# Zero rows added to the mixer's narrow stationary operands, and a sample state update split by sequence

## The chip, the cores and the metric

One core of a Trainium2 chip runs the whole program. The metric is the device time of one execution in microseconds (us). The engines are TensorE (PE; its weight loads have a row of their own, PEld), VectorE (DVE), ScalarE (ACT), GpSimd (POOL) and SyncE (SP, which issues most DMAs).

## The reference, cut to what matters

One layer of a hybrid decoder runs for a prompt of 1024 tokens (with 16 meta tokens before it) and for 8 sample sequences of 8 tokens. Around the part that changes lie two large feed-forward blocks. The mixer between them has two branches over the same projected input. Branch A is a gated delta rule with 8 heads of 128 x 128 state:

```
def gated_delta_recurrent(q, k, v, beta, g, s0):          # the 8 sample sequences
    def step(s, xs):
        q_t, k_t, v_t, b_t, g_t = xs
        s = s * jnp.exp(g_t)[..., None, None]
        u = b_t[..., None] * (v_t - jnp.einsum('nhd,nhde->nhe', k_t, s))
        s = s + k_t[..., :, None] * u[..., None, :]
        return s, jnp.einsum('nhd,nhde->nhe', q_t, s)
```

The prompt does the same in chunks. Branch B is attention in a window of 128 tokens, where every query also sees the 16 meta keys:

```
o = (jnp.einsum('nbkgqs,nskd->nbqkgd', p[..., :N_META], v_meta)
     + jnp.einsum('nbkgqs,nskd->nbqkgd', p[..., N_META:], vb))       # prompt
o = (jnp.einsum('nkgts,nskd->ntkgd', p[..., :N_META], v_meta)
     + jnp.einsum('nkgts,nskd->ntkgd', p[..., N_META:], v_all))      # samples
```

The outputs are the two results and the new states, among them the sample states after 8 steps for each head and sequence.

## The kernel before, in words

Tokens lie in 9 tiles: 8 of 128 prompt tokens and one of 80 (64 sample tokens, 16 meta tokens). A matmul has a stationary operand of rows x columns (rows are the contraction, held on partitions) and a moving operand that streams through it; the profile writes `48*128 48x256` for 48 rows, 128 columns and 256 moving columns. Operands typed float32r take one pass, float32 ones take two passes, so they appear twice for each call. The large projections split each operand into a high and a low part and make three products (lines L128, L130, L132).

The order of TensorE's instructions is written out by hand: `weave` deals the steps of several generators into one sequence, so that attention blocks or the delta chain lie between steps of a projection. A step is one product of a projection or the stretch of a generator up to its next `yield`. The other engines and the DMA queues are ordered by a planner that simulates the program.

Stages that the change touches, with times of the profile:

- **Window attention, about 1010 to 1330 us.** `window` runs 32 blocks (4 head pairs x 8 tiles), each in `swa_block`, among projections (`swa_q`, later `qv_steps`). In the first two of the four pairs every tenth projection step also lets DVE do a step of the triangular solve (`lane_solve`, L1061 and L1063). In a block the probabilities of the meta keys come in three parts of 16 rows (high, low, high); they are transposed (L1233), copied to `pm` (L1235) and multiplied by `vm`, three times 16 meta values (L1162), as the first product of the group at L1256. Both operands have 48 rows. Sample attention (`swa_sample`, twice, in two halves each) multiplies four sequences per half: for each of four column strips a product with 128 cache rows (L1313) and one with 24 rows of meta and own values (L1314), into the same 32 output rows.
- **Delta heads, about 1345 to 1890 us.** For each head, `chain` first treats the sample tile and then eight prompt tiles, woven with projections, with `prep` and `prep8` of the next head and with `emit` of the one before. In `prep8` the sample keys and queries are packed into `kq` and multiplied (L1504, 64 columns stationary); `kd8`, the decayed keys of the 80 tokens, is loaded (L1490). In `chain`, 16 meta rows of `kd8` start the prompt state (L1551); `p8` of 64 rows gives the sample outputs (L1554), which `normed` writes to rows 64 to 127 of `on8`; POOL writes `xe` (L1561), the solved sample values masked into eight sequences; and after tiles 1 and 3 a product with 64 rows of `kd8` and 512 moving columns of `xe` (L1602) gives the update of four sequence states, which DVE adds (L1604). `emit` transposes the outputs (L1619), for the samples with 64 rows.

Of the kernel before, what the change touches and what calls it, by code (L numbers as in the profile page):

```python
# [649 lines left out]
H = 8  # L650
C_IDENT, C_TRI, C_TRI8, C_BLK8, C_TRIQ, C_MNEG, C_MNEG8 = (i * P for i in range(7))
C_SMASK = 7 * P
C_BASE = C_SMASK + 8
C_BASE0 = C_BASE + 272
C_SBIAS = C_BASE0 + 144
C_W = C_SBIAS + 304
# [2 lines left out]
def constants():  # L659

    r = np.arange(P)
    seq = np.where(r < 64, r // 8, np.where(r < 80, 8, -1))
    live = (r < 80)
    same = (seq[:, None] == seq[None, :]) & live[:, None] & live[None, :]
    le = r[:, None] <= r[None, :]
    cst = np.zeros((P, C_W), np.float32)
    cst[:, C_IDENT:C_IDENT + P] = np.eye(P)
    cst[:, C_TRI:C_TRI + P] = le
    cst[:, C_TRI8:C_TRI8 + P] = le & same
    cst[:, C_BLK8:C_BLK8 + P] = same  # L670
    cst[:64, C_TRIQ + 64:C_TRIQ + P] = (le & same)[:64, :64]
    cst[:, C_MNEG:C_MNEG + P] = np.where(le, 0.0, NEG)
    cst[:, C_MNEG8:C_MNEG8 + P] = np.where(le & same, 0.0, NEG)
    cst[:64, C_SMASK:C_SMASK + 8] = seq[:64, None] == np.arange(8)[None, :]
    i, k = r[:, None], r[None, :]
    own = np.where(k <= i, k - i, NEG)
    cst[:, C_BASE:C_BASE + P] = np.where(k >= i, k - i - P, NEG)
    cst[:, C_BASE + P:C_BASE + 144] = -P
    cst[:, C_BASE + 144:C_BASE + 272] = own
    m = np.arange(16)[None, :]  # L680
    cst[:, C_BASE0:C_BASE0 + 16] = -np.minimum(16 + i - m, P)
    cst[:, C_BASE0 + 16:C_BASE0 + 144] = own
    row_h, row_t = (r % 32) // 8, r % 8
    for g in range(2):
        slope = 2.0 ** -(4 * g + row_h + 1.0)
        d = np.concatenate([
            np.where(k >= row_t[:, None], P - k + row_t[:, None], -NEG),
            np.full((P, 16), float(P)),
            np.where(np.arange(8)[None, :] <= row_t[:, None], row_t[:, None] - np.arange(8)[None, :], -NEG)], 1)
        cst[:, C_SBIAS + g * 152:C_SBIAS + (g + 1) * 152] = -slope[:, None] * d  # L690
    return cst


class Mixer:
    def __init__(self, c, xT, I, O, es, ba_w):
# [7 lines left out]
        self.ek = ExitStack()  # L703
        self.pcp, self.pcs = c.pool(self.ek, "mpc", side="right"), 3
        t = lambda shape, tag, dt=F32: c.t(kp, shape, dt, tag=tag)
        self.smask = t([P, 8], "smask")
        nc.sync.dma_start(self.smask, I["cst"][:, C_SMASK:C_SMASK + 8])
        self.cw = t([P, 24, 4], "cw")
        nc.sync.dma_start(self.cw, I["dn_conv_w"])
        self.hist = t([P, 24, 24], "hist")  # L710
# [102 lines left out]
    def gates(self, tp):  # L813
# [31 lines left out]
        for m in (15, 13, 11, 9, 7, 5, 3):  # L845
# [5 lines left out]
        nc.vector.scalar_tensor_tensor(out=g, in0=x, scalar=-1.0, in1=bc(ea), op0=ALU.mult, op1=ALU.mult)  # L851
        g8x = c.t(tp, [80, 8, H], tag="g8x")
        nc.vector.tensor_tensor(out=g8x, in0=g[:80, 8, :].unsqueeze(1).to_broadcast([80, 8, H]),
                                in1=self.smask[:80].unsqueeze(2).to_broadcast([80, 8, H]), op=ALU.mult)
        yield

        pg = self.ps([P, 4, 72], "tr", 3)
# [242 lines left out]
    def swa_kv(self, pool, tmp):  # L1100
# [3 lines left out]
        self.kn = c.t(pool, [P, 2, 64], tag="kn")  # L1104
        self.vt = [c.t(pool, [P, 8, 256], F32R, tag=f"vt{x}") for x in "hl"]
        vt = c.t(tmp, [P, 2, 256], tag="vtok")
        self.vm = c.t(pool, [48, 256], F32R, tag="vm")
        self.scst = c.t(pool, [P, C_W - C_BASE], tag="scst")
        nc.sync.dma_start(self.scst, self.I["cst"][:, C_BASE:])
        ktok = c.t(tmp, [P, 2, 256], tag="ktok")  # L1110
# [47 lines left out]
        vm = c.t(tmp, [P, NTOK], tag="fm", bufs=2)[0:48, 0:256]  # L1158
        for i in (0, 16, 32):
            nc.sync.dma_start(vm[i:i + 16], vt[64:80, 1, :])  # L1160
        nc.vector.tensor_copy(self.vm, vm)
        nc.vector.tensor_tensor(out=self.vm[32:48], in0=vm[32:48], in1=f32(self.vm[32:48]), op=ALU.subtract)  # L1162

    def swa_q(self, h):
# [32 lines left out]
    def swa_block(self, t, p, pool):  # L1197
# [33 lines left out]
        pt = self.ps([P, 4, P], "pt", 2)  # L1231
        for i in range(2):
            nc.tensor.transpose(pt[:48, i, :], f32(m3[:, i]).rearrange("p a k -> p (a k)"), self.k(C_IDENT))  # L1233
        pm = c.t(pool, [48, 2, P], F32R, tag="ptm", bufs=2)
        nc.scalar.copy(pm, pt[:48, 0:2])  # L1235
        ops, late = [(self.vm[:, gs], pm)], []
        yield
        parts = [(own, t, "pto")]
# [31 lines left out]
    def swa_sample(self, g, pool, tmp):  # L1270
# [25 lines left out]
        for half in range(2):  # L1296
            h4 = slice(4 * half, 4 * half + 4)
            vc = c.t(tmp, [P, 4, 152], tag="kc")[:, :, 0:P]
            v24 = c.t(tmp, [24, 4, P], tag="v24")
            nc.sync.dma_start(vc, I["cache_swa_v"][0, h4, :, g].rearrange("s w d -> w s d"))  # L1300
            nc.sync.dma_start(v24[0:16], I["cache_swa_meta_v"][0, h4, :, g].rearrange("s m d -> m s d"))
            nc.sync.dma_start(v24[16:24], self.vn_d[32 * half:32 * half + 32, gs].rearrange("(s t) e -> t s e", t=8))
            pt = self.ps([P, 4, P], "pt", 2)
            nc.tensor.transpose(pt[:, 0, :], s[:, half, 0:P], self.k(C_IDENT))
            nc.tensor.transpose(pt[:24, 1, :], s[:, half, P:152], self.k(C_IDENT))
            p = c.t(tmp, [P, 2, P], tag="pts")
            nc.scalar.copy(p[:, 0], pt[:, 0])
# [12 lines left out]
            sv = sg[:, :, 32 * half:32 * half + 32].rearrange("p h (s t) -> p h s t", t=8)  # L1320
            nc.vector.tensor_tensor(out=sv, in0=sv, in1=px.rearrange("p (s h t) -> p h s t", h=4, t=8), op=ALU.mult)
            yield
# [83 lines left out]
    def persistent(self, pool):  # L1406
        c, nc = self.c, self.nc
        self.ms = [c.t(pool, [P, 8, P], tag=f"ms{i}") for i in range(1)]
        self.p8 = [c.t(pool, [64, P], tag=f"p8{i}") for i in range(2)]
        for m in self.ms + self.p8:  # L1410
            nc.gpsimd.memset(m, 0.0)

    def prep(self, h, g, pool):
# [66 lines left out]
    def prep8(self, h, pool):  # L1480
# [5 lines left out]
        nc.sync.dma_start(kq[:, 0:64], self.kf_d[h][:, 1024:1088])  # L1486
        dt8 = T([64, 64], "dt8")
        nc.sync.dma_start(dt8, self.dt_d[h][0:64, 8, 0:64])
        kd = x["kd8"] = T([P, P], "kd8")
        nc.sync.dma_start(kd, self.kd_d[h][:, 8, :])  # L1490
        s0 = x["s0"] = T([P, 8, P], "s0")
        self.pack8(kq[:, 64:P], x["qv"], meta=False)

        ms = x["ms"] = self.ms[0]
        for half in range(2):
# [5 lines left out]
        nc.sync.dma_start(s0, I["state_dn_ssm"][0, :, h].rearrange("s k v -> k s v"))  # L1501
        p8 = x["p8"] = self.p8[h % 2]
        pk = self.ps([P, 4, P], "tr")
        nc.tensor.matmul(pk[:64, 0, 0:64], kq[:, 0:64], kq[:, 64:P], start=True, stop=True)  # L1504
        nc.vector.scalar_tensor_tensor(out=p8[:, 64:P], in0=pk[:64, 0, 0:64], scalar=self.s[:64, h, 8:9], in1=dt8,
                                       op0=ALU.mult, op1=ALU.mult)
        yield
        x8 = T([P, 80], "v8")
# [7 lines left out]
    def chain(self, h, pool):  # L1516
# [1 line left out]
        c, nc = self.c, self.nc  # L1518
        T = lambda shape, tag, bufs=None, dt=F32: c.t(pool, shape, dt, tag=tag, bufs=bufs)
        x = self.hd[h]  # L1520
        vs, kd, s0, ms, p8 = (x[k] for k in ("vs8", "kd8", "s0", "ms", "p8"))
        so = T([P, 9], "so", 2)
        x["on"] = []

# [12 lines left out]
        for i in range(8):  # L1537
# [10 lines left out]
        yield  # L1548
        S = T([P, P], "S", 3)
        pu = self.ps([P, P], "ch", 2)  # L1550
        nc.tensor.matmul(pu, kd[64:80], xs8[64:80], start=True, stop=True)  # L1551
        nc.scalar.copy(S, pu)
        po = self.ps([P, P], "oq")
        nc.tensor.matmul(po, p8, xs8[0:64], start=True, stop=True)  # L1554
        o = T([P, P], "o", 2)
        nc.vector.tensor_tensor(out=o[64:P], in0=po[64:P], in1=qs8[64:P], op=ALU.add)
        on = T([P, 1, P], "on8")
        normed(o, slice(64, P), 8, 0, on)
        x["on"].append((on, 8, 1, 64))
        xe = T([64, 8, P], "xe")  # L1560
        nc.gpsimd.tensor_tensor(out=xe, in0=xs8[0:64].unsqueeze(1).to_broadcast([64, 8, P]),  # L1561
                                in1=self.smask[:64].unsqueeze(2).to_broadcast([64, 8, P]), op=ALU.mult)
        nc.gpsimd.tensor_tensor(out=s0, in0=s0, in1=self.csx[:, :, h].unsqueeze(2).to_broadcast([P, 8, P]), op=ALU.mult)
        yield
        for t in range(8):
# [33 lines left out]
            if t in (1, 3):  # L1599
                half = t // 2  # L1600
                pu = self.ps([P, 4, P], "on")
                nc.tensor.matmul(pu, x["kd8"][0:64], xe[:, 4 * half:4 * half + 4, :], start=True, stop=True)  # L1602
                sl = s0[:, 4 * half:4 * half + 4, :]
                nc.vector.tensor_tensor(out=sl, in0=sl, in1=pu, op=ALU.add)  # L1604
                if half:
                    nc.sync.dma_start(self.O["s_ssm"][0, :, h].rearrange("s k v -> k s v"), s0)
                yield
        nc.sync.dma_start(self.O["p_ssm"][0, 0, h], S)

    def emit(self, h, pool):  # L1610
# [4 lines left out]
        for on, t0, n, w in x["on"]:  # L1615
            pt = self.ps([P, 4, P], "on")
            for i in range(n):
                r = slice(0, P) if w == P else slice(64, P)
                nc.tensor.transpose(pt[:, i, :w], on[r, i, :], self.k(C_IDENT)[r, r])  # L1619
            zc = Z[:, t0 * P:t0 * P + n * w].rearrange("p (i w) -> p i w", w=w)  # L1620
            nc.vector.scalar_tensor_tensor(out=zc, in0=pt[:, :n, :w], scalar=self.nw, in1=zc, op0=ALU.mult,
                                           op1=ALU.mult)
            cols = slice(t0 * P, t0 * P + n * w)
            yw = self.c.t(pool, [P, 512], tag="yw", bufs=1)
# [516 lines left out]
```

## Time and profile before

| | us |
|---|---|
| median of 3 runs | 2738.6 (2738.1 to 2738.87) |
| the profiled execution | 2743.03 |
| its span, first to last instruction | 2741.2 |
| mean granted TensorE clock | 0.984 of full speed |

The span is what the trace shows; 1.8 us of the profiled execution's time lie around it, and it took 4.4 us more than the median of the runs. Times in rows are counted from the span's start.

### The profile page before, as it was taken

How to read it: one execution, taken by the hardware profiler on the slowest of the kernel's cores; microseconds unless marked ns; L12 is line 12 of the kernel's file. 1: busy time of each engine (PE TensorE's matmuls, PEld its weight loads, DVE VectorE, ACT ScalarE, POOL GpSimd, SP SyncE). 2: the span in 40 equal slices, each digit the busy share in tenths (PEclk: the TensorE clock that was granted, in tenths of full speed). 3: DMA queues.
4: the chain of work that ended last, by engine and by line, in shares of the span. 5: the costliest groups of instructions: out<-in, count | busy, mean ns of one | idle time of the engine just before them, and what ended most of it. 6: DMA issues, size and time to landing. Idle time of an engine off the chain costs nothing. (4 is left out here: it accounts for less than half of the span.)

```text
span 2741.2 us, 49395 instructions
## 1 busy us (share of the span) xinstructions
PE 2654.0 (97%) x18957; PEld 2491.2 (91%) x18957; DVE 1587.4 (58%) x2396; ACT 1086.3 (40%) x2579; POOL 1359.7 (50%) x1283
## 2 busy tenths in 40 slices
PE   7999999999989998999999999998999999999998
PEld 7999999999988997887788888886789999999998
DVE  7656566446657679945454444443556566563566
ACT  6333343422146723354444444444443343344221
POOL 6656555445326735644344433444455555554462
PEclk9999999999999999999999999999999999999999
DMA  4344343676434643354333333334434344338764
GB/s 163 115 151 163 121 150 125 252 235 237 169 124 162 225 135 107 104 178 114 81 97 97 96 90 97 92 98 136 133 132 143 124 148 151 131 133 302 241 237 141
DMA packets 229554, 406.48 MB, mean 148 GB/s; under 512 B 59734, under 2 KB 121334, under 8 KB 229030
## 3 DMA queue, kind: packets, MB, share of 16 engines
q1 hardware_dynamic: 209014, 324.75, 36.8%
q10 hardware_dynamic: 20304, 78.56, 7.2%
q8 instruction: 150, 2.46, 0.4%
q14 instruction: 86, 0.70, 0.1%
HBM read 264.36 MB, written 140.53 MB: 148 GB/s over the span
## 5 line engine op out<-in xcount | busy, mean ns | idle before, releaser
L132 PE MATMUL gu<-xh,wl 128*128 128x512 f32 (+3 forms) x1456 | 498.5, 342 | 0.9 <-POOL wl L764 0.9
L128 PE MATMUL gu<-xh,wh 128*128 128x512 f32 (+3 forms) x1456 | 494.9, 340 | 0.0
L130 PE MATMUL gu<-xl,wh 128*128 128x512 f32 (+3 forms) x1456 | 494.5, 340 | 0.0
L282 POOL TENSOR_TENSOR wl<-T,wh 128x512 fp32r<-128x512 f32 x246 | 330.9, 1351 | 323.3 <-ACT wh L281 244.4
L492 PE MATMUL y<-hb,wh 128*128 128x256 f32 (+2 forms) x2528 | 432.0, 290 | 5.9 <-DMA hb<-hid 3.9
L282 POOL TENSOR_TENSOR wl<-raw,wh 128x512 fp32r<-128x512 f32 x200 | 280.7, 1411 | 257.7 <-ACT wh L281 202.8
L492 PEld LDWEIGHTS y<-hb,wh 128*128 128x128 f32 x2528 | 367.0, 189 | 7.9 <-DMA hb<-hid 4.9
L132 PEld LDWEIGHTS gu<-xh,wl 128*128 128x128 f32 x1456 | 279.2, 192 | 29.4 <-issue 11.1
L281 ACT CAST wh<-T 128x512 fp32r<-128x512 f32 x246 | 152.4, 620 | 368.9 <-PE B L316 115.9
L130 PEld LDWEIGHTS gu<-xl,wh 128*128 128x128 f32 x1456 | 279.2, 192 | 18.9 <-issue 1.2
L128 PEld LDWEIGHTS gu<-xh,wh 128*128 128x128 f32 x1456 | 279.1, 192 | 18.3 <-issue 1.6
L492 PE MATMUL y<-hb,wl 128*128 128x256 f32 (+2 forms) x1264 | 272.5, 289 | 0.0
L281 ACT CAST wh<-raw 128x512 fp32r<-128x512 f32 x200 | 122.2, 620 | 275.6 <-PE C L316 84.1
L503 DVE TENSOR_TENSOR acc<-acc,y 128x552 f32<-128x552 f32 (+4 forms) x216 | 144.6, 678 | 142.2 <-PE y L492 141.9
L764 POOL TENSOR_TENSOR wl<-raw,wh 128x1024 fp32r<-128x1024 f32 x60 | 147.7, 2462 | 139.2 <-ACT wh L763 119.0
L492 PEld LDWEIGHTS y<-hb,wl 128*128 128x128 f32 x1264 | 207.7, 189 | 0.4 <-POOL wl L282 0.4
L256 DVE TENSOR_TENSOR T<-raw,raw 128x512 f32<-128x512 f32 x124 | 118.4, 959 | 115.5 <-POOL wl L282 115.5
L1532 POOL TENSOR_TENSOR f<-f,mhalf 128x1 f32<-128x1 f32 (+1 forms) x72 | 54.5, 757 | 113.8 <-DVE f L1530 104.4
L267 DVE TENSOR_TENSOR T<-raw,T 128x512 f32<-128x512 f32 x62 | 64.4, 1041 | 64.2 <-POOL wl L282 64.1
L256 DVE TENSOR_TENSOR T<-raw,T 128x512 f32<-128x512 f32 x62 | 64.2, 1044 | 33.3 <-POOL wl L282 33.1
L922 DVE SCALAR_TENSOR_TENSOR cv<-pc,cw,cv 128x1131 f32<-128x1131 f32 x48 | 66.9, 1396 | 27.0 <-POOL cv L919 26.7
L1061 DVE TENSOR_TENSOR ltmp<-la 72x14 f32<-72x14 f32 (+37 forms) x76 | 70.8, 932 | 12.4 <-DMA la<-b_d 11.1
(594 smaller groups left out, 7389.3 us busy)
## 6 DMA issues: line engine op xcount, KB each, us to landing
hb<-hid SPq DMA_DIRECT2D x71, 552.0 KB
hb<-hid SPq DMA_DIRECT2D x71, 544.0 KB
hid<-hs ACTq DMA_DIRECT2D x69, 552.0 KB
hid<-hs ACTq DMA_DIRECT2D x69, 544.0 KB
raw<-in_w_in_dram SPq DMA_DIRECT2D x58, 512.0 KB
raw<-in_ffn_w_gate_dram SPq DMA_DIRECT2D x100, 256.0 KB
raw<-in_ffn_w_up_dram SPq DMA_DIRECT2D x94, 256.0 KB
raw<-in_ffn_w_down_dram SPq DMA_DIRECT2D x88, 256.0 KB
```

The source lines that it names most:

```text
L128: nc.tensor.matmul(ps, wh, xh, start=first and i == 0, stop=False)
L130: nc.tensor.matmul(ps, wh, xl, start=False, stop=False)
L132: nc.tensor.matmul(ps, wl, xh, start=False, stop=last and i == n - 1)
L256: pin(self.nc.vector.tensor_tensor(out=b[name], in0=b[x], in1=b[y], op=ALU.subtract))
L267: nc.vector.tensor_tensor(out=s, in0=b["21"], in1=s, op=ALU.subtract)
L281: self.nc.scalar.copy(hi, s)
L282: self.nc.gpsimd.tensor_tensor(out=lo, in0=s, in1=f32(hi), op=ALU.subtract)
L492: self.nc.tensor.matmul(self.view(ps[d], (i,)), w[x][:, d * P:(d + 1) * P], hb[:, y, lo:hi], start=j + x + y == 0, stop=j == len(items) - ...
L503: dve = lambda out, x, y: nc.vector.tensor_tensor(out=out, in0=x, in1=y, op=ALU.add)
L764: nc.gpsimd.tensor_tensor(out=lo, in0=raw, in1=f32(hi), op=ALU.subtract)
L922: nc.vector.scalar_tensor_tensor(out=cv, in0=pc[:, w:w + PADW], scalar=self.cw[:, j, w:w + 1], in1=cv, op0=ALU.mult, op1=ALU.add)
L1061: nc.vector.tensor_tensor(out=t, in0=a[:n, 0:j, j:j + 1].to_broadcast([n, j, w]), in1=a[:n, j:j + 1, j + 1:size].to_broadcast([n, j, w]), ...
```

## The change

Stationary operands with 16, 24, 48 or 64 rows are treated so that they have 80 or 128 rows, or so that they stand together.

- `vm` and `pm` become tiles of 128 rows that are set to zero once; the copies fill 48 rows, and the product at L1256 uses all 128. `pm` is two fixed tiles, taken by tile parity, in place of a pool tile with two buffers.
- In `swa_sample` the four products with 24 rows follow the four with 128 rows, in place of alternating with them. They are not filled up.
- The sample tile: `p8` has 80 rows (the last 16 zero); the product of keys and queries uses all 128 columns of `kq` as the stationary operand; `on8` is one fixed tile of 128 rows with zeros above, and its transpose uses all of it.
- The state update: `xe` goes. In `prep8` POOL writes `kds`, nine masked copies of `kd8` (eight sequences and the meta tokens) of 80 rows. L1551 uses copy 8, and each L1602 becomes four products, one for each sequence, with the same moving operand `xs8` of 128 columns. The mask in the constants gets a ninth column.

```
-        self.vm = c.t(pool, [48, 256], F32R, tag="vm")
+        self.vm = c.t(pool, [P, 256], F32R, tag="vm")
+        self.pm = [c.t(pool, [P, 2, P], F32R, tag=f"ptm{i}") for i in range(2)]
+        for x in (self.vm, *self.pm):
+            nc.gpsimd.memset(f32(x), 0.0)
...
-        pm = c.t(pool, [48, 2, P], F32R, tag="ptm", bufs=2)
-        nc.scalar.copy(pm, pt[:48, 0:2])
+        pm = self.pm[t % 2]
+        nc.scalar.copy(pm[0:48], pt[:48, 0:2])
...
                 nc.tensor.matmul(po[r], p[:, 0, r], vc[:, i, :], start=True, stop=False, tile_position=(0, 32 * i))
+            for i in range(4):
+                r = slice(32 * i, 32 * i + 32)
                 nc.tensor.matmul(po[r], p[:24, 1, r], v24[:, i, :], start=False, stop=True, tile_position=(0, 32 * i))
...
-        self.p8 = [c.t(pool, [64, P], tag=f"p8{i}") for i in range(2)]
+        self.p8 = [c.t(pool, [80, P], tag=f"p8{i}") for i in range(2)]
+        self.on8 = c.t(pool, [P, 1, P], tag="on8")
...
-        kd = x["kd8"] = T([P, P], "kd8")
+        kd = T([P, P], "kd8")
         nc.sync.dma_start(kd, self.kd_d[h][:, 8, :])
+        kds = x["kds"] = T([80, 9, P], "kds")
+        nc.gpsimd.tensor_tensor(out=kds, in0=kd[:80].unsqueeze(1).to_broadcast([80, 9, P]),
+                                in1=self.smask[:80].unsqueeze(2).to_broadcast([80, 9, P]), op=ALU.mult)
...
-        nc.tensor.matmul(pk[:64, 0, 0:64], kq[:, 0:64], kq[:, 64:P], start=True, stop=True)
+        nc.tensor.matmul(pk[:, 0, 0:64], kq, kq[:, 64:P], start=True, stop=True)
...
-        nc.tensor.matmul(pu, kd[64:80], xs8[64:80], start=True, stop=True)
+        nc.tensor.matmul(pu, kds[:, 8], xs8[:80], start=True, stop=True)
...
-        nc.tensor.matmul(po, p8, xs8[0:64], start=True, stop=True)
+        nc.tensor.matmul(po, p8, xs8[:80], start=True, stop=True)
...
-        xe = T([64, 8, P], "xe")
-        nc.gpsimd.tensor_tensor(out=xe, in0=xs8[0:64].unsqueeze(1).to_broadcast([64, 8, P]),
-                                in1=self.smask[:64].unsqueeze(2).to_broadcast([64, 8, P]), op=ALU.mult)
...
-                nc.tensor.matmul(pu, x["kd8"][0:64], xe[:, 4 * half:4 * half + 4, :], start=True, stop=True)
+                for s in range(4):
+                    nc.tensor.matmul(pu[:, s, :], kds[:, 4 * half + s], xs8[:80], start=True, stop=True)
...
-                r = slice(0, P) if w == P else slice(64, P)
-                nc.tensor.transpose(pt[:, i, :w], on[r, i, :], self.k(C_IDENT)[r, r])
+                nc.tensor.transpose(pt[:, i, :], on[:, i, :], self.k(C_IDENT))
```

## Rows read from the trace of the kernel before

**Rows 1.** The page: busy time, share of the span and instructions of each engine.

```profile
PE 2654.0 (97%) x18957; PEld 2491.2 (91%) x18957; DVE 1587.4 (58%) x2396; ACT 1086.3 (40%) x2579; POOL 1359.7 (50%) x1283
```

**Rows 2.** Stretches: length, busy PE, PEld, DVE, ACT, POOL, clock, DMA.

```profile
1052.00:1150.00 98.00, 88.34 (x532) 77.01 (x531) 96.49 (x163) 35.61 (x110) 63.08 (x62) 0.97 0.34 102
1150.00:1330.00 180.00, 175.29 (x1097) 145.39 (x1097) 101.21 (x273) 83.97 (x253) 82.94 (x128) 0.98 0.43 131
1416.00:1487.00 71.00, 71.00 (x472) 62.49 (x471) 31.90 (x66) 31.11 (x101) 28.59 (x36) 1.00 0.33 94
```

**Rows 3.** Longest of PE's waits from 1150 to 1330: total us, times, longest.

```profile
PE pt L1244 <- ACT ptm L1235: 3.3, 4, 1.9
```

**Rows 4.** Timeline of PE, a meta product: start us, us, line, names, shapes.

```profile
1061.53 0.28 PE L128 MATMUL gu<-xh,wh 128*128 128x256 f32 x1
1061.65 0.28 PE L130 MATMUL gu<-xl,wh 128*128 128x256 f32 x1
1061.86 0.38 PE L1256 MATMUL po<-ptm,vm 48*128 48x256 f32 x1
1062.17 0.39 PE L1256 MATMUL po<-ptoh,vth 128*128 128x256 f32 x1
1062.39 0.27 PE L1256 MATMUL po<-ptoh,vtl 128*128 128x256 f32 x1
```

**Rows 5.** Line L1256 from 1052 to 1150: ns min/median/max, first and last start.

```profile
L1256 PE MATMUL po<-ptm,vm x9: 379/382/383, 1061.9 to 1141.5; 48*128 48x256 f32 x9
```

**Rows 6.** Timeline of PE, sample scores (L1289) and sample values (L1313, L1314).

```profile
1201.81 0.47 PE L1289 MATMUL sc<-kc,qp 128*32 128x152 f32 x8
1202.20 0.41 PE L128 MATMUL gu<-xh,wh 128*128 128x320 f32 x1
...
1219.22 0.41 PE L1313 MATMUL po<-kc,pts 128*32 128x128 f32 x2
...
1221.89 0.41 PE L128 MATMUL gu<-xh,wh 128*128 128x320 f32 x1
```

**Rows 7.** Timeline of PE, eight full passes (L1463), then a state update (L1602).

```profile
1368.78 0.39 PE L130 MATMUL gu<-xl,wh 128*128 128x512 f32 x1
1369.02 1.05 PE L1463 MATMUL tr<-qv,kf 128*128 128x128 f32 x8
...
1370.14 0.40 PE L128 MATMUL gu<-xh,wh 128*128 128x512 f32 x1
...
1370.70 1.12 PE L1602 MATMUL on<-xe,kd 64*128 64x512 f32 x2
...
1372.09 0.40 PE L128 MATMUL gu<-xh,wh 128*128 128x512 f32 x1
```

**Rows 8.** Timeline of PE, keys times queries of a sample tile (L1504).

```profile
1463.32 0.39 PE L130 MATMUL gu<-xl,wh 128*128 128x512 f32 x1
1463.64 0.33 PE L1504 MATMUL tr<-kq 128*64 128x64 f32 x2
...
1464.23 0.39 PE L128 MATMUL gu<-xh,wh 128*128 128x512 f32 x1
```

**Rows 9.** Timeline of PE, a product of 80 rows, then of 16 and 64.

```profile
1484.65 0.39 PE L132 MATMUL gu<-xh,wl 128*128 128x512 f32 x1
1484.88 0.38 PE L1545 MATMUL ch<-vs,r 80*80 80x128 f32 x2
...
1485.33 0.39 PE L130 MATMUL gu<-xl,wh 128*128 128x512 f32 x1
...
1487.19 0.28 PE L128 MATMUL gu<-xh,wh 128*128 128x256 f32 x1
1487.40 0.48 PE L1551 MATMUL ch<-xs,kd 16*128 16x128 f32 x2
...
1488.45 0.28 PE L132 MATMUL gu<-xh,wl 128*128 128x256 f32 x1
```

**Rows 10.** Groups of POOL, 1345 to 1900: count, busy us, mean ns, idle before.

```profile
L1561 POOL TENSOR_TENSOR xe<-xs,smask 64x1024 f32<-64x1024 f32 x8 | 15.1, 1892 | 6.9 <-ACT xs L1547 6.9
```

More of the change, by code (lines that the diff above doesn't have):

```diff
@@ L652 @@
 C_SMASK = 7 * P
-C_BASE = C_SMASK + 8
+C_BASE = C_SMASK + 16
 C_BASE0 = C_BASE + 272
@@ L673, in constants @@
     cst[:, C_MNEG8:C_MNEG8 + P] = np.where(le & same, 0.0, NEG)
-    cst[:64, C_SMASK:C_SMASK + 8] = seq[:64, None] == np.arange(8)[None, :]
+    cst[:80, C_SMASK:C_SMASK + 9] = seq[:80, None] == np.arange(9)[None, :]
     i, k = r[:, None], r[None, :]
@@ L705, in __init__ @@
         t = lambda shape, tag, dt=F32: c.t(kp, shape, dt, tag=tag)
-        self.smask = t([P, 8], "smask")
-        nc.sync.dma_start(self.smask, I["cst"][:, C_SMASK:C_SMASK + 8])
+        self.smask = t([P, 9], "smask")
+        nc.sync.dma_start(self.smask, I["cst"][:, C_SMASK:C_SMASK + 9])
         self.cw = t([P, 24, 4], "cw")
@@ L853, in gates @@
         nc.vector.tensor_tensor(out=g8x, in0=g[:80, 8, :].unsqueeze(1).to_broadcast([80, 8, H]),
-                                in1=self.smask[:80].unsqueeze(2).to_broadcast([80, 8, H]), op=ALU.mult)
+                                in1=self.smask[:80, 0:8].unsqueeze(2).to_broadcast([80, 8, H]), op=ALU.mult)
         yield
@@ L1160, in swa_kv @@
             nc.sync.dma_start(vm[i:i + 16], vt[64:80, 1, :])
-        nc.vector.tensor_copy(self.vm, vm)
+        nc.vector.tensor_copy(self.vm[0:48], vm)
         nc.vector.tensor_tensor(out=self.vm[32:48], in0=vm[32:48], in1=f32(self.vm[32:48]), op=ALU.subtract)
@@ L1408, in persistent @@
         self.ms = [c.t(pool, [P, 8, P], tag=f"ms{i}") for i in range(1)]
-        self.p8 = [c.t(pool, [64, P], tag=f"p8{i}") for i in range(2)]
-        for m in self.ms + self.p8:
+        self.p8 = [c.t(pool, [80, P], tag=f"p8{i}") for i in range(2)]
+        self.on8 = c.t(pool, [P, 1, P], tag="on8")
+        for m in (*self.ms, *self.p8, self.on8):
             nc.gpsimd.memset(m, 0.0)
@@ L1503, in prep8 @@
         pk = self.ps([P, 4, P], "tr")
-        nc.tensor.matmul(pk[:64, 0, 0:64], kq[:, 0:64], kq[:, 64:P], start=True, stop=True)
-        nc.vector.scalar_tensor_tensor(out=p8[:, 64:P], in0=pk[:64, 0, 0:64], scalar=self.s[:64, h, 8:9], in1=dt8,
+        nc.tensor.matmul(pk[:, 0, 0:64], kq, kq[:, 64:P], start=True, stop=True)
+        nc.vector.scalar_tensor_tensor(out=p8[:64, 64:P], in0=pk[:64, 0, 0:64], scalar=self.s[:64, h, 8:9], in1=dt8,
                                        op0=ALU.mult, op1=ALU.mult)
@@ L1520, in chain @@
         x = self.hd[h]
-        vs, kd, s0, ms, p8 = (x[k] for k in ("vs8", "kd8", "s0", "ms", "p8"))
+        vs, kds, s0, ms, p8 = (x[k] for k in ("vs8", "kds", "s0", "ms", "p8"))
         so = T([P, 9], "so", 2)
@@ L1550, in chain @@
         pu = self.ps([P, P], "ch", 2)
-        nc.tensor.matmul(pu, kd[64:80], xs8[64:80], start=True, stop=True)
+        nc.tensor.matmul(pu, kds[:, 8], xs8[:80], start=True, stop=True)
         nc.scalar.copy(S, pu)
         po = self.ps([P, P], "oq")
-        nc.tensor.matmul(po, p8, xs8[0:64], start=True, stop=True)
+        nc.tensor.matmul(po, p8, xs8[:80], start=True, stop=True)
         o = T([P, P], "o", 2)
         nc.vector.tensor_tensor(out=o[64:P], in0=po[64:P], in1=qs8[64:P], op=ALU.add)
-        on = T([P, 1, P], "on8")
-        normed(o, slice(64, P), 8, 0, on)
-        x["on"].append((on, 8, 1, 64))
-        xe = T([64, 8, P], "xe")
-        nc.gpsimd.tensor_tensor(out=xe, in0=xs8[0:64].unsqueeze(1).to_broadcast([64, 8, P]),
-                                in1=self.smask[:64].unsqueeze(2).to_broadcast([64, 8, P]), op=ALU.mult)
+        normed(o, slice(64, P), 8, 0, self.on8)
+        x["on"].append((self.on8, 8, 1, 64))
         nc.gpsimd.tensor_tensor(out=s0, in0=s0, in1=self.csx[:, :, h].unsqueeze(2).to_broadcast([P, 8, P]), op=ALU.mult)
@@ L1617, in emit @@
             for i in range(n):
-                r = slice(0, P) if w == P else slice(64, P)
-                nc.tensor.transpose(pt[:, i, :w], on[r, i, :], self.k(C_IDENT)[r, r])
+                nc.tensor.transpose(pt[:, i, :], on[:, i, :], self.k(C_IDENT))
             zc = Z[:, t0 * P:t0 * P + n * w].rearrange("p (i w) -> p i w", w=w)
-            nc.vector.scalar_tensor_tensor(out=zc, in0=pt[:, :n, :w], scalar=self.nw, in1=zc, op0=ALU.mult,
+            nc.vector.scalar_tensor_tensor(out=zc, in0=pt[:, :n, P - w:], scalar=self.nw, in1=zc, op0=ALU.mult,
                                            op1=ALU.mult)
```

## The prediction

> **What bounds the kernel now.** I read the page first: TensorE is busy for 97% of the span, and no other engine comes near [rows 1]. But an average says nothing of the two stages that change, so the windows came next [rows 2]. In a head of the delta stage PE is busy for 71.00 of 71 us, and POOL for 28.59. That stage is PE's, and what its instructions cost is paid in full. From 1150 to 1330, in window attention, PE has 175.29 of 180 us, and the 4.7 us left are waits on the blocks' own small work, the longest group 3.3 us [rows 3]. From 1052 to 1150 it is otherwise: DVE has 96.49 of 98 us and PE 88.34. There the triangular solve on DVE sets the pace, and PE time that is saved turns mostly into waiting.
>
> Busy PE is not useful PE, so the third view is the timeline around the instructions that the diff touches, read by starts, not by durations. In a run of 256-column products the starts are 0.12 us apart (0.117 over several; 512 columns take twice that, 0.235). The 48-row product at L1256 starts 0.21 us after the product before it, the next one 0.31 us later, the third 0.22 us later [rows 4]. Three intervals that should be 0.35 us together are 0.74 us. So at each change from a full operand to a narrow one and back, PE first lets the product in flight finish (0.09 us) and then loads weights in the open (0.10 us), which otherwise pass under the product before. A product of 80 rows does not do that: L1545 starts 0.23 us after a 512-column product, which is the plain cadence [rows 9]. And eight full passes of 128 columns with eight different operands (L1463) take 1.36 us with a 512-column product on either side; less 2 x 0.235, that is 0.89 us, 0.11 us for each, with the loads hidden [rows 7]. These three readings carry the forecast: the price hangs on the operand's shape, 80 or 128 rows pay none of it, 16, 24, 48 and 64 rows do.
>
> **The change, part by part.**
>
> *Meta product (L1256), 32 blocks.* After the change it is one more 256-column product among full ones: 0.74 - 3 x 0.117 = 0.39 us saved a block [rows 4]. Nine blocks lie in the stretch that DVE bounds [rows 5]: 3.5 us on PE, between 0 and 3.5 in the time; I take a quarter, 0.9, since PE is not idle everywhere there. The other 23 give 9.0 us.
>
> *Sample values (L1313, L1314), 4 halves.* Now the shape changes with every pair of passes, and a half takes 1221.89 - 1219.22 = 2.67 us [rows 6]. Sorted, there is one change inside. What four products of one shape in four column strips cost is shown by the sample scores (L1289): eight passes in 0.39 us [rows 6], much less than eight times 0.11, so the strips run at the same time. Two such groups: 0.8 us, saving 1.87 a half, 7.5 us. The lower bound is that the 24-row group, or both, run one pass after another: then only six of eight changes go, each worth 2.67 / 8 - 2 x 0.11 = 0.11 us, 2.7 us in all. I take 7.5, as L1313 has L1289's very shape.
>
> *Start state and sample outputs (L1551, L1554), 8 heads.* 1488.45 - 1487.19 = 1.26 us, less 2 x 0.117 for the two projection products, is 1.03 us [rows 9]. Four full passes take 4 x 0.11 = 0.45. Saved 0.58 x 8 = 4.6 us.
>
> *State update (L1602), 16 times.* From 1370.14 to 1372.09 are 1.95 us; less 3 x 0.235, 1.245 us [rows 7]. Afterwards eight passes of 128 columns, the number and shape of L1463: 0.89. Four times the loads and the same columns: saved 0.355 x 16 = 5.7 us.
>
> This is where a rule of the Trainium skill speaks against the change. L1463 shows eight loads of full 128-row operands hidden under full products. The page "TensorE: Matmul & The Clock Gate", Part 3, "The mechanism", says that a weight load overlaps a running matmul only when it goes to another row group; by that, full operands would never hide a load, and the eight passes would each pay the open load. The trace does not agree: 0.11 us a pass [rows 7].
>
> *Keys times queries (L1504), 8 heads.* 0.91 - 2 x 0.235 = 0.44 us [rows 8]. A pair of passes with a wide operand is L1545's 0.68 - 0.47 = 0.21 [rows 9]. Saved 0.23 x 8 = 1.8 us.
>
> *Output transpose (L1619), 8 heads.* It stands ahead of 64-row products of `prep` that stay, so one change of shape of two goes, 0.1 us as in [rows 4]; 0.8 us.
>
> *POOL.* `xe` goes (1.89 us for 1024 elements, 8 times [rows 10]); `kds` has 1152, so 2.13 us, placed in `prep8`. POOL is idle for 42 of 71 us in a head [rows 2], which hides it. Without that cover it would add 0.24 us a head, 1.9 us. `kds` waits for its load and, having one buffer, for the last L1602 of the head before; behind it in POOL's queue stand the next low weight halves (L764), the edges of the convolution input (L899) and the output factors (L1532). The weights are made one column ahead: a column is 24 products over 1104 tokens, 24 x 1104 x 0.117 / 256 = 12.1 us of PE. So a wait of a few us stops nobody. The DMAs stay the same in number and, but for a column of the mask, in size; the load at L1490 no longer waits for L1602 to release `kd8`, so nothing behind it on SP gets later. The three memsets at the start of window attention are at most a quarter of `xe` each, 0.5 us, once; taken as 0, likewise the second of them being late for a first block.
>
> *Sum.* 9.0 + 0.9 + 7.5 + 4.6 + 5.7 + 1.8 + 0.8 = 30.3 us. Against it I set new waits in window attention: PE arrives earlier at products that follow ACT and DVE. Their bounds are 0 and what the 23 blocks save, 9.0; the existing waits of that kind are 3.3 us [rows 3], and I take two thirds as much again, 2.3. Net 28.0 us. The profiled execution had 2741.2 us of span and 1.8 around it, 2743.0; it becomes 2715.0. It lay 4.4 above the median of the runs, so the median goes from 2738.6 to **2710.6 us**.
>
> **The rivals.**
>
> 1. *The sorted sample products do not overlap.* For it: L1314's 24 rows with 32 columns appear nowhere in an unbroken run. Against it: L1289. Gain 28.0 - 4.8 = 23.2, time 2715.4.
> 2. *Window attention is not PE's after 1150 either*, the blocks' chain (transposes, copies, products) keeps its length, and the blocks' saving becomes waiting. For it: the group of 3.3 us is such a chain. Against it: 175.29 of 180. The gain loses the blocks' net share, 9.0 + 0.9 - 2.3 = 7.6: 28.0 - 7.6 = 20.4, time 2718.2. With rival 1 as well, 2723.0.
> 3. *The four products of an update load in the open*, each pass waiting for its 128 rows as the third product in [rows 4] does, 0.10 us. Eight passes, 16 updates: 12.8 us back, time 2723.4. L1463 in [rows 7] speaks against it. The Trainium skill's rule above would give this case.
> 4. *Zero rows do not spare the pause*, which would then follow from something other than the row count; 2738.6. L1545 speaks against it, but it is one shape with 80 columns.
> 5. *Slower: POOL held by `kds`.* The planner may queue it ahead of work that PE needs, while it waits for its load or for the earlier head's L1602. It decides once POOL is held longer than the 12.1 us by which weights lead: to cost more than 28.0 + 5.5 us over 8 heads, PE must stop 4.2 us a head, POOL be held 16 us. At 20 us a head the loss is 8 x 7.9 = 63 us, net 35 slower, 2774. The 42 idle us a head speak against it.
>
> **How the numbers follow.** Forecast 0.58, rival 1 0.15, rival 2 0.14, both 0.03, rival 3 0.03, rival 4 0.03, rival 5 0.04. About 0.2% (5.5 us) is what a measurement of this kernel can tell from no change. All but the last two lie beyond it: faster 0.93, same 0.03, slower 0.04. The range runs from 2705 (no new waits and the nine early blocks kept: 30.3 + 2.6 = 32.9 us) to 2724 (rivals 1 and 2 together, rival 3), and leaves out rivals 4 and 5 and some 0.05 of tails.
>
> **What would show it.** Right: around L1256, L1551, L1554, L1504 and L1602 starts at plain cadence; L1602 as eight passes in 0.9 us; a half of the sample values in 0.8 us; a head, about 71 us, shortened by 1.6; PE with more idle time from 1052 to 1150, and little more after. Wrong: pauses that stay at 80 or 128 rows, L1313 and L1314 0.11 us apart pass by pass, PE waiting on ACT or DVE in blocks for as long as it saved, or waits on POOL `wl` or `kds`. The forecast falls above all if new waits in the blocks exceed 9 us.

## The result, and the profile after

| | us |
|---|---|
| before, median of 4 runs beside these | 2738.35 |
| after, median of 4 runs (2721.54 to 2729.78) | 2724.39 |
| ratio, 95% interval | 0.9945 [0.9925, 0.9965] |
| profiled execution after (its span) | 2724.97 (2723.1) |
| forecast | 2710.6 (2705 to 2724) |

The change gained 14.0 us where 28.0 were forecast. The median lies 0.4 us beyond the slow end of the range; by the ratio, 0.9945 of 2738.6 is 2723.5, just inside it. Single runs of one kernel lie several us apart (the kernel before: 2731 to 2748 in 21 runs beside the first experiments), so I read medians, and stretches of one trace.

The page of the kernel after, its busy line, then the stretches of [rows 2] in the same columns:

```profile
PE 2620.6 (96%) x19053; PEld 2495.4 (92%) x19053; DVE 1593.1 (59%) x2396; ACT 1084.0 (40%) x2579; POOL 1367.8 (50%) x1287
```

```profile
1052.00:1150.00 98.00, 87.81 (x536) 79.94 (x537) 97.46 (x165) 37.11 (x114) 62.52 (x59) 0.93 0.32 95
1150.00:1330.00 180.00, 168.62 (x1195) 149.09 (x1193) 103.47 (x279) 88.54 (x269) 87.29 (x139) 1.00 0.49 146
1416.00:1487.00 71.00, 69.44 (x481) 63.61 (x480) 32.73 (x67) 30.82 (x101) 28.59 (x36) 1.00 0.31 91
```

PE's busy time fell by 33.4 us and the span by 18.1: PE does less and waits more. In the head stage, where it had been busy for 71.00 of 71 us [rows 2], it now idles 1.56. The rows of 1150 to 1330 are not alike: the kernel after enters its heads about 18 us earlier.

The edited products themselves, on PE's timeline of the kernel after (line numbers have moved: L1256 is L1260, L1313 and L1314 are L1317 and L1320, L1504 is L1515, L1551 and L1554 are L1562 and L1565, L1602 is L1610):

```profile
1057.79 0.28 PE L130 MATMUL gu<-xl,wh 128*128 128x256 f32 x1
1057.91 0.28 PE L1260 MATMUL po<-ptm,vm 128*128 128x256 f32 x1
1058.03 0.28 PE L1260 MATMUL po<-ptoh,vth 128*128 128x256 f32 x1
1058.14 0.28 PE L1260 MATMUL po<-ptoh,vtl 128*128 128x256 f32 x1
...
1213.06 0.42 PE L1317 MATMUL po<-kc,pts 128*32 128x128 f32 x8
1213.41 0.42 PE L1320 MATMUL po<-v,pts 24*32 24x128 f32 x8
1213.76 0.41 PE L128 MATMUL gu<-xh,wh 128*128 128x320 f32 x1
...
1446.73 0.39 PE L130 MATMUL gu<-xl,wh 128*128 128x512 f32 x1
1446.96 0.33 PE L1515 MATMUL tr<-kq 128*128 128x64 f32 x2
...
1447.42 0.39 PE L128 MATMUL gu<-xh,wh 128*128 128x512 f32 x1
...
1470.23 0.28 PE L128 MATMUL gu<-xh,wh 128*128 128x256 f32 x1
1470.35 0.38 PE L1562 MATMUL ch<-xs,kds 80*128 80x128 f32 x2
...
1470.91 0.28 PE L132 MATMUL gu<-xh,wl 128*128 128x256 f32 x1
...
1487.75 0.40 PE L128 MATMUL gu<-xh,wh 128*128 128x512 f32 x1
...
1488.21 1.05 PE L1610 MATMUL on<-xs,kds 80*128 80x128 f32 x8
...
1489.34 0.28 PE L128 MATMUL gu<-xh,wh 128*128 128x256 f32 x1
```

Read by starts as in the forecast, and against [rows 4, 6 to 9]: the meta product and the two behind it start 0.12 us apart (0.74 us became 0.35). A half of the sample values takes 13.76 - 13.06 = 0.70 us instead of 2.67; both groups overlap, the 24-row one too. L1515 takes 0.69 - 2 x 0.235 = 0.22, L1562 and L1565 together 0.68 - 2 x 0.117 = 0.45, a state update 1.59 - 3 x 0.235 = 0.885 (a product or two of a projection is left out at each "..."). Each is within 0.1 us of its forecast. How the price that went divides into a pause ahead of a narrow operand and an open load behind it (0.09 and 0.10 us in the forecast), no run shows. The loss is elsewhere.

PE's longest waits from 1410 to 1870, in the kernel after: total us, times, longest.

```profile
PE ch L1588 <- DVE b L1580: 9.7, 7, 1.6
PE ch L1593 <- ACT xs L1590: 5.3, 4, 2.3
```

Before, the same view has no row at all. But that kernel runs some 18 us later, and the waits on `xs`, at the end of the last head, lie behind its window; from 1870 to 1900 it has them:

```profile
PE ch L1586 <- ACT xs L1583: 4.0, 4, 2.0
```

So the waits on `b` are what is new. Here are the timelines of POOL and of DVE, in the kernel after, just ahead of one such wait (start us, us, line):

```profile
1431.35 1.76 POOL L1543 TENSOR_TENSOR f<-f,mhalf 128x1 f32<-128x1 f32 x1
1433.08 2.11 POOL L1500 TENSOR_TENSOR kds<-kd,smask 80x1152 f32<-80x1152 f32 x1
```

```profile
1431.29 1.40 DVE L922 SCALAR_TENSOR_TENSOR cv<-pc,cw,cv 128x1131 f32<-128x1131 f32 x1
1432.61 0.68 DVE L1612 TENSOR_TENSOR s<-s,on 128x512 f32<-128x512 f32 x1
1433.20 3.18 DVE L922 SCALAR_TENSOR_TENSOR cv<-pc,cw,cv 128x1131 f32<-128x1131 f32 x1
1436.30 0.68 DVE L1382 SCALAR_TENSOR_TENSOR Z<-tz,gu 128x512 f32<-128x512 f32 x1
1436.90 0.34 DVE L1580 SCALAR_TENSOR_TENSOR b<-ch,ne,vs 128x128 f32<-128x128 f32 x1
```

`kds` starts 0.12 us ahead of a convolution tap (L922), and the tap takes 3.18 us instead of 1.39: what is left of `kds`, 1.99, and then nearly its own time. Behind the tap in DVE's queue stands `b`, for which PE waits 1.56 us. The first row of each timeline shows the opposite order: another tap starts first, and POOL's one-column `f` takes 1.76 us instead of 0.55. By these times, the one that starts later stands still until the other is done.

Six of the 48 taps on values are held up, which one line of the groups tells (count, busy us, mean ns, idle before); its mean before was 1396 ns:

```profile
L922 DVE SCALAR_TENSOR_TENSOR cv<-pc,cw,cv 128x1131 f32<-128x1131 f32 x48 | 77.6, 1619 | 27.3 <-POOL cv L919 27.0
```

At the first boundary between heads `kds` (for head 1) costs in another way. It stands in POOL's own queue ahead of the first tap on values, which POOL does itself (L919). POOL's timeline:

```profile
1365.91 2.13 POOL L1500 TENSOR_TENSOR kds<-kd,smask 80x1152 f32<-80x1152 f32 x1
...
1368.28 1.26 POOL L919 TENSOR_SCALAR cv<-pc,cw 128x1131 f32<-128x1131 f32 x1
```

DVE's three taps behind it keep their 1.39 us, but they and the packing of the values come some 2 us late. PE waits 1.87 us for `v`, and behind that gap its granted clock falls: in the stretches below it is 0.73 and 0.58 of full speed on average, between its two levels of 2.4 and 1.2 GHz (kernel after, columns as above).

```profile
1376.00:1381.00 5.00, 3.13 (x19) 2.58 (x17) 2.47 (x5) 1.59 (x7) 0.60 (x3) 0.73 0.05 10
1381.00:1386.00 5.00, 5.00 (x28) 4.51 (x27) 0.35 (x1) 2.17 (x7) 0.44 (x1) 0.58 0.30 77
```

A head's length can be read from POOL's first tap on values (L919: ns min/median/max, first and last start of six, five heads apart), before:

```profile
L919 POOL TENSOR_SCALAR cv<-pc,cw x6: 1231/1236/1238, 1448.0 to 1804.2; 128x1131 f32<-128x1131 f32 x6
```

And after:

```profile
L919 POOL TENSOR_SCALAR cv<-pc,cw x6: 1234/1234/1234, 1430.0 to 1787.6; 128x1131 f32<-128x1131 f32 x6
```

356.2 / 5 = 71.24 us a head before, 357.6 / 5 = 71.52 after. With fewer PE microseconds in it, a head became longer by 0.28 us.

### The profile page after: what moved, and what is told of

It is laid out like the page before. It is cut to its first block, busy times and chain, and to the rows that moved or that the text cites. A ratio compares the mean times of both kernels' runs of the same rounds, so it can differ in the third digit from the quotient of the medians.

```text
span 2723.1 us, 49595 instructions
## 1 busy us (share of the span) xinstructions
PE 2620.6 (96%) x19053; PEld 2495.4 (92%) x19053; DVE 1593.1 (59%) x2396; ACT 1084.0 (40%) x2579; POOL 1367.8 (50%) x1287
## 5 line engine op out<-in xcount | busy, mean ns | idle before, releaser
L764 POOL TENSOR_TENSOR wl<-raw,wh 128x1024 fp32r<-128x1024 f32 x60 | 146.9, 2448 | 131.6 <-ACT wh L763 112.9
L922 DVE SCALAR_TENSOR_TENSOR cv<-pc,cw,cv 128x1131 f32<-128x1131 f32 x48 | 77.6, 1619 | 27.3 <-POOL cv L919 27.0
L763 ACT CAST wh<-raw 128x1024 fp32r<-128x1024 f32 x60 | 62.9, 1048 | 33.6 <-PE gu L130 32.1
```

What stands on the lines that cost most here:

```text
L764: nc.gpsimd.tensor_tensor(out=lo, in0=raw, in1=f32(hi), op=ALU.subtract)
L922: nc.vector.scalar_tensor_tensor(out=cv, in0=pc[:, w:w + PADW], scalar=self.cw[:, j, w:w + 1], in1=cv, op0=ALU.mult, op1=ALU.add)
```

## The experiments

**Theory.** What PE saves is real everywhere. In the heads it is lost because `kds` runs on POOL beside DVE taps whose operands all lie in SBUF, and holds them up. **Rivals.** A: products with filled-up operands do not pay in the heads. B: PE arrives earlier at a chain of unchanged length, and would wait with or without `kds`.

| kernel | median us | less before | ratio, 95% | us a head |
|---|---|---|---|---|
| window attention only | 2720.67 | -16.1 | 0.9937 [0.9924, 0.9949] | 71.2 |
| heads only | 2740.77 | +4.0 | 1.0014 [1.0005, 1.0023] | 71.5 |
| sorting only | 2728.5 | -9.7 | 0.996 [0.9948, 0.9973] | |
| meta products only | 2730.13 | -8.1 | 0.9976 [0.9964, 0.9987] | |
| before + a POOL product | 2741.73 | +4.9 | 1.0007 [0.9995, 1.0019] | 71.8 |
| `kds` later on POOL | 2711.9 | -26.3 | 0.9905 [0.9892, 0.9918] | 69.8 |
| values masked, no `kds` | 2708.65 | -28.1 | 0.9893 [0.9879, 0.9906] | 69.8 |
| the same + POOL product | 2719.46 | -18.3 | 0.9934 [0.992, 0.9947] | 70.8 |
| the same + POOL fills | 2709.05 | -28.7 | 0.9893 [0.9879, 0.9906] | 69.8 |
| `kds` on ACT | 2721.18 | -17.0 | 0.9935 [0.9922, 0.9947] | 69.9 |

### The change in two halves

The first kernel has the edits of `vm`, `ptm` and of the sample value loop, and the heads of before.

> Only the window-attention part of the change (zero-filled meta operands of 128 rows, sample value products sorted by shape); the heads are those of the kernel before. Theory (the PE terms are real, the heads lost theirs because POOL's kds runs beside DVE's convolution taps and holds them up): about 15 to 17 us faster than before, 2722 to 2724, nearly all that the whole change gave. Rival A (part of what window attention gains is only moved and is given back at the next stage): under 10 us, 2729 or more. Rival B (the gain in window attention needs nothing of the heads, and the heads' wait comes from PE arriving earlier at a chain of unchanged length): the same as the theory, and then PE waits of about 1.5 us a head at the product that reads b, though kds is not there.

The second has the heads' edits, and window attention as before.

> Only the heads' part of the change (kds, 80-row operands, eight masked key products, wide keys times queries, output transpose). My forecast's own terms: 12.9 us faster, 2725.5. Theory (kds beside the convolution): the 12.9 us are eaten by six waits of about 1.6 us and by the stall at the first boundary of about 5, so 2736 to 2742, and six PE waits of about 1.5 us on b. Rival A (these products do not save what their shapes promise): 2736 to 2742 too, but without the waits: the starts around the edited products then stand as far apart as before.

Measured: -16.1 and +4.0. Window attention alone gives at least what the whole change gave (the intervals of the two ratios overlap). The heads' part costs time where 12.9 us of gain were forecast, so some 17 us are lost there; its trace has nine waits on `b` from 1326 to 1900, 10.9 us, and the same 71.5 us a head. The first kernel waits on `b` once, for 1.0 us. That the products save what their shapes promise was read above, so rival A falls here.

### Window attention's two terms

```diff
             for i in range(4):
                 r = slice(32 * i, 32 * i + 32)
                 nc.tensor.matmul(po[r], p[:, 0, r], vc[:, i, :], start=True, stop=False, ...)
+            for i in range(4):
+                r = slice(32 * i, 32 * i + 32)
                 nc.tensor.matmul(po[r], p[:24, 1, r], v24[:, i, :], start=False, stop=True, ...)
```

> The kernel before with the sample value products sorted by shape and nothing else. My forecast's term: 7.5 us (two groups of four products that overlap); its lower bound, were they to run one after another, 2.7 us. Theory: 7 to 8 us faster than before. If sorting alone gives little, the gain of window attention is the meta product's.

The other kernel has the edits of `vm` and `ptm` alone:

> The kernel before with the meta products' operands filled up to 128 rows and nothing else. My forecast's terms: 9.0 + 0.9 - 2.3 = 7.6 us faster. With nothing lost to new waits 9 to 10; if the blocks' chain sets the pace (my second rival) 0 to 2.

Measured -9.7 and -8.1, 17.8 together beside 16.1 for both at once and 15.1 in the forecast. The two terms hold, sorting a little more than forecast; the second rival of the forecast, by which the meta products would give nothing, falls.

### One more POOL product in the kernel before

```diff
         kd = x["kd8"] = T([P, P], "kd8")
         nc.sync.dma_start(kd, self.kd_d[h][:, 8, :])
+        ex = T([80, 8, P], "ex")
+        nc.gpsimd.tensor_tensor(out=ex, in0=kd[:80].unsqueeze(1).to_broadcast([80, 8, P]),
+                                in1=self.smask[:80].unsqueeze(2).to_broadcast([80, 8, P]), op=ALU.mult)
```

> The kernel before and nothing of the change, but for one more POOL product a head (80 rows by 1024, keys by mask, read by nobody) at the place where kds stands in the changed kernel. Theory: DVE's tap beside it takes about 3 us instead of 1.4, b comes about 1.6 us later, PE waits 1 to 1.6 us in each of six heads and up to 5 us at the first boundary: 8 to 15 us slower, 2746 to 2753. Rival B (early arrival of PE): no change, 2736 to 2741, since PE is not faster here. A smaller loss would say that PE has slack before b in the kernel before.

Measured +4.9 by the medians and 1.9 by the ratio, whose interval holds no change. That is less than the 8 to 15 expected, and the times alone do not decide between the theory and no change. The trace does. At 1454.21 the tap starts first, keeps its 1.39 us, and the POOL product takes 2.79 instead of 1.90; that head has its 71.2 us. In the later heads the product meets the third tap, not the second (DVE's timeline of this kernel):

```profile
1525.44 3.10 DVE L922 SCALAR_TENSOR_TENSOR cv<-pc,cw,cv 128x1131 f32<-128x1131 f32 x1
1528.47 0.33 DVE L1591 SCALAR_TENSOR_TENSOR S<-S,cdec,ch 128x128 f32<-128x128 f32 x1
```

The four heads that can be measured with a held tap are 72.0 us long, 0.75 more than before. Before, PE started the product that reads `b` 0.88 us after the `b` behind the third tap was ready, and 0.38 us after the one behind the second; the spare time covers part of the 1.7 us. So PE's early arrival (rival B) has this much truth: it takes away spare time. That it makes no wait by itself the next runs show.

### The same `kds`, later in POOL's queue

```diff
-        kds = x["kds"] = T([80, 9, P], "kds")
-        nc.gpsimd.tensor_tensor(out=kds, ...)
...
         nc.scalar.activation(vs[:80], pt[:80, 0, :], AF.Copy, scale=self.nr[:80, h, 8:9])
+        kds = x["kds"] = T([80, 9, P], "kds")
+        c.tc.keep_in_program_order(nc.gpsimd.tensor_tensor(out=kds, ...))
```

The second copy of the values' packing (L935) is pinned in order too, so that `kds` stays behind it.

> The whole change, with kds still on POOL and still 2.1 us long, but queued from the second head on behind the packing of the values, after the convolution's last DVE operation; for head 0 its place stays. Theory (kds beside a DVE tap whose operands all lie in SBUF holds it up, nothing else is wrong with it): the six waits of 1.56 us go, the stall at the first boundary and what follows it (some 5 us) stays: 9 to 11 us faster than the changed kernel, 22 to 26 faster than before. Rival (it is the length of POOL's queue or kds's own lateness that costs): no better than the changed kernel, 12 to 16 us faster than before.

Measured -26.3, just above the 22 to 26 expected: I had taken the `kds` of the first boundary for head 0's, but it is head 1's and moved as well. So this run takes away both costs at once, the held taps and the late tap of POOL. POOL does the same work as in the changed kernel, 69.8 us a head, and the taps are whole again (groups of DVE):

```profile
L922 DVE SCALAR_TENSOR_TENSOR cv<-pc,cw,cv 128x1131 f32<-128x1131 f32 x48 | 67.0, 1397 | 29.5 <-POOL cv L919 29.2
```

PE's waits on `b` from 1410 to 1870 are 0.3 us in all, though PE arrives as early as in the changed kernel. Rival B falls as the cause of the 1.56 us.

### Values masked instead of keys

```diff
-        kds = x["kds"] = ... (on POOL)
+        kdm = x["kdm"] = T([80, P], "kdm")
+        nc.scalar.activation(kdm, kd[:80], AF.Copy, scale=self.smask[:80, 8:9])
...
-        nc.tensor.matmul(pu, kds[:, 8], xs8[:80], start=True, stop=True)
+        nc.tensor.matmul(pu, kdm, xs8[:80], start=True, stop=True)
...
+        xe = T([80, 8, P], "xe")
+        nc.gpsimd.tensor_tensor(out=xe, in0=xs8[:80]..., in1=self.smask[:80, 0:8]..., op=ALU.mult)
...
-                for s in range(4):
-                    nc.tensor.matmul(pu[:, s, :], kds[:, 4 * half + s], xs8[:80], start=True, stop=True)
+                nc.tensor.matmul(pu, x["kd8"][:80], xe[:, 4 * half:4 * half + 4, :], start=True, stop=True)
```

> The whole change but for kds: POOL masks the new values (80 rows instead of 64) at the old place in the chain, the state update is one 512-column product of 80 rows for a half, and the start state reads one masked copy of the keys that ACT makes. Theory: no DVE tap takes 3 us, no PE wait of 1.5 us on b; the heads then give 4.6 + 1.8 + 0.8 us and for the update 16 x (1.245 - 0.47) = 12.4, together 19.6, beside 16 in window attention: about 35 us faster, 2701 to 2708. Rival B (PE arrives earlier at a chain of unchanged length): the wait on b stays at 1.5 us a head or grows, 2714 to 2722. Rival A (80 rows of zeros do not pay in the heads): 2720 to 2724.

Measured -28.1: no held tap, no wait on `b` over 0.2 us, and, with the kernel of the fills further down, the fastest here. The time lies 0.7 us above the 2701 to 2708 expected. The expectation overrated one term. From PE's timeline of this kernel:

```profile
1483.20 0.40 PE L128 MATMUL gu<-xh,wh 128*128 128x512 f32 x1
...
1483.67 1.02 PE L1612 MATMUL on<-xe,kd 80*128 80x512 f32 x2
...
1484.77 0.28 PE L128 MATMUL gu<-xh,wh 128*128 128x256 f32 x1
```

1.57 - 3 x 0.235 = 0.865 us for the two passes, not 0.47: a pass of 512 columns of this product costs four of 128. So one product with 80 rows takes what eight masked passes take (0.885), against 1.245 with 64 rows [rows 7]. The gain of the state update lies in the rows of the operand, not in cutting it up, and the eight masked products were not needed.

### POOL's product put back, and fills in its place

Into the last kernel, at the place of `kds`, goes its product again, read by nobody, and in the second kernel a copy of one column and two fills:

```diff
+        ex = T([80, 9, P], "ex")
+        nc.gpsimd.tensor_tensor(out=ex, in0=kd[:80]..., in1=self.smask[:80]..., op=ALU.mult)
```

```diff
+        ex = T([P, 9, P], "ex")
+        nc.gpsimd.tensor_copy(ex[:, 0, 0:1], kd[:, 0:1])
+        nc.gpsimd.memset(ex, 0.0)
+        nc.gpsimd.memset(ex, 0.0)
```

> The version with masked values (28 us faster than before), and kds's product put back on POOL at kds's place, read by nobody. Theory: that op alone is what parts the changed kernel from this version: the tap of 3.18 us and six waits of about 1.5 us come back, 9 us, and at the first boundary some 2 to 5 more: 12 to 19 us faster than before. Rival (the eight masked key products as such, or their 80-row loads, were dearer than the one product): 26 to 29 us faster, the op costs nothing.

> The same with POOL busy at the same place for about the same 2 us, but with two fills (128 x 1152 zeros each, after a copy of one column), which read nothing. Theory in its narrow form (POOL holds a DVE tap up only while it reads SBUF itself): taps of 1.4 us, no waits, 26 to 29 us faster than before. Rival (any POOL work at this place costs it, through POOL's queue or through writes): as with the product, 12 to 19.

Measured -18.3 and -28.7. The product by itself takes 10 us away, the fills nothing. The waits on `b` do not come back as expected: from 1410 to 1870 they are 4.2 us, the longest 0.8, and a head has 70.8 us, since the product waits for its load there and meets a later tap than `kds` did. At the first boundary both kernels have the same order, which is not that of the changed kernel: POOL's tap comes first, and DVE's first tap starts 0.1 us behind the added work. With the product, DVE's timeline:

```profile
1370.29 3.23 DVE L922 SCALAR_TENSOR_TENSOR cv<-pc,cw,cv 128x1131 f32<-128x1131 f32 x1 [1.32 <-POOL cv L919]
```

With the fills, the timelines of POOL and then of DVE:

```profile
1369.49 1.07 POOL L1502 MEMSET ex<- 128x1152 f32 x1
1370.62 1.06 POOL L1503 MEMSET ex<- 128x1152 f32 x1
```

```profile
1369.33 1.40 DVE L922 SCALAR_TENSOR_TENSOR cv<-pc,cw,cv 128x1131 f32<-128x1131 f32 x1 [1.31 <-POOL cv L919]
...
1371.11 1.39 DVE L922 SCALAR_TENSOR_TENSOR cv<-pc,cw,cv 128x1131 f32<-128x1131 f32 x1
```

Two taps keep their 1.4 us beside the fills. In the later heads the one-column copy itself waits for the tap (1.41 us instead of 0.21), so the fills there stand beside L926, which keeps its 1.34 us too.

### `kds` on ACT

```diff
+        for s in range(9):
+            nc.scalar.activation(kds[:, s], kd[:80], AF.Copy, scale=self.smask[:80, s:s + 1])
```

> The whole change, with kds made on ACT by nine copies of 80 x 128, each scaled by one column of the mask; POOL has neither kds nor the masked values. Theory: all of the heads' 12.9 us comes out, also at the first boundary: about 28 us faster than before, if ACT's nine copies (some 2 us a head on an engine that is 40% busy) delay nothing that PE waits for; 26 to 29. Rival (the heads' wait is PE arriving too early at a chain of unchanged length): 14 to 18.

Measured -17.0, outside what the theory expected, though the heads have their 69.9 us and `b` costs little. The loss is at the entry of head 0. ACT's timeline there:

```profile
1320.76 2.73 ACT L1501 ACTIVATE kds<-kd,smask 80x128 f32<-80x128 f32 x9
1323.39 1.11 ACT L1455 ACTIVATE vs<-tr,nr__1447_9680 128x128 f32<-128x128 f32 x4
```

The nine copies take 2.73 us and stand ahead of the scaled values, for which PE waits 2.5 us. Behind that gap the granted clock is at the lower of its two levels, 0.50 or 1.2 GHz (stretches of this kernel, columns as before):

```profile
1320.00:1325.00 5.00, 2.38 (x16) 1.80 (x16) 0.15 (x1) 4.06 (x16) 0.00 (x0) 0.95 0.68 155
1325.00:1335.00 10.00, 8.40 (x36) 7.26 (x35) 1.57 (x6) 2.59 (x10) 0.00 (x0) 0.50 0.43 110
1335.00:1340.00 5.00, 5.00 (x25) 4.33 (x23) 0.83 (x2) 1.15 (x4) 2.96 (x2) 0.68 0.24 52
```

Ten us at 0.50 and five at 0.68 are at most 6.6 us lost, since PE was idle for part of them; with the wait, 9.1. The three fast kernels gain 9 to 12 us more. The trace is that of the slowest of this kernel's six executions (2715.86 to 2724.68), so the split is one of that execution and not of the median. ACT's idle time was another cover that was not there, not a mark against the theory.

## Why the forecast was half right

That the time came out at the slow end of the range is luck. That end was worked out from rivals 1 and 2 together, or rival 3, and none of them came true; what cost the 14 us stood in the sum as nothing.

- *The price of a narrow operand* was right, and so was every term by its shape: 0.39 us a meta product, 1.97 us a half of the sample values (forecast 1.87), 0.58, 0.36 and 0.22 us in the heads. The output transpose (0.8 us) was not looked at by itself. The kernel with masked values gains 28.1 us, the forecast's 28.0, with all of its terms but another route for the update; the heads' share in it, 28.1 - 16.1 = 12.0, answers to 12.9. That the sum agrees to 0.1 us is luck in part, as the two shares miss by about 1 us each, in opposite directions.
- *Window attention* gave 16.1, forecast 15.1. The waits of [rows 3] grew from 3.3 to 5.3 us, by 2.0, where 2.3 had been set.
- *Rivals 1 to 4* fell: the sample products overlap, the blocks pay, the state update's loads are hidden (0.11 us a pass), and zeros do spare the pause. For the loads, one sentence of the Trainium skill's "TensorE: Matmul & The Clock Gate", Part 3, "The mechanism" (an overlap only with another row group), would have had every pass pay its own; this trace does not agree with it, at 0.885 us for eight. The same section also has loads pulled ahead into a background weight buffer, which the forecast did not weigh and which fits these 0.885 us.
- *Rival 5* named the right instruction. Its way needed POOL held for 16 us, and `kds` takes 2.1. In the six later heads nothing behind it in POOL's queue was late; at the first boundary POOL's tap was, by some 2 us, so in small that way is one part of the loss.
- **The step that failed** is POOL's: "POOL is idle for 42 of 71 us in a head [rows 2], which hides it." An idle share of POOL tells neither what stands behind an instruction in its queue at that moment nor what DVE runs beside it. `kds` replaced `xe`, of almost the same length, but beside seven of the eight `xe` DVE ran nothing at all, and six of the `kds` ran beside a tap. Price: 71.52 - 69.78 = 1.74 us a head, six times 10.4, for the held taps; for the late tap at the first boundary waits of 1.87 and 0.53 us, and 5 x 0.27 + 5 x 0.42 = 3.5 us by the clock, an upper bound since PE was idle for part of it. The clock's part is read from one execution. Together up to 16.3, where 14.1 part the changed kernel from the masked values.
- The trace of before held the warning. A POOL `f` of 0.55 us takes 1.76 there beside a tap; DVE's own one-column `f` (L1530) takes 2.2 us there, at 1407.95, beside a low weight half of POOL (L764), where 0.16 is its usual time. I had read POOL's rows for length and order, and not beside DVE's.

The Trainium skill states the rule in "SBUF — State Buffer", "Who interferes with whom": a DVE instruction with two SBUF inputs contends with a GpSimd instruction that reads SBUF, not with one that only writes, and the one that starts later stands still to the end of the first. The trace agrees on each point: 3.18 and 3.23 us behind a product, 1.39 and 1.40 beside fills, 2.79 on POOL where the tap came first.

## What to carry to other kernels

A stationary operand filled up with zeros to the row count of its neighbours can be worth far more than the columns it costs, but price such an edit by starts, beside the products it will stand among. Before an instruction goes to POOL, ask what DVE runs at that moment and where its operands lie, and what stands behind it in POOL's queue; the idle share of POOL answers neither. Where the collision is found, move the instruction, or use a form that does not read SBUF.

## What the runs showed of the hardware that I had not expected

- A DVE instruction with one of its two operands in PSUM ran beside the same kind of POOL product at full speed: in the kernel after, the state (L1595) started 13 times while POOL worked on a low weight half (L764, 2.4 us) and took its usual 0.35 us, where a tap with all operands in SBUF needed 3.18 beside `kds`.
- A 24-row group of four products in four column strips overlapped like one of 128 rows: 0.35 us for eight passes.
- A PE gap of 1.87 us was followed by 5 us at a mean granted clock of 0.58 in one kernel, and one of 2.5 us by 10 us at 0.50 in another (the levels are 2.4 and 1.2 GHz). Not every such gap was: behind the six waits of 1.56 us in the kernel after, and behind one of 1.9 us near 1871 in the kernel with the fills, the clock stayed at 1.00. By the estimates above, a wait with a fall behind it cost up to three or four times its own length.
